# The last weight group, two stage borders and the order of weight splits in a float32 streaming block

## The chip, the cores and the metric

The kernel runs on one core of one Trainium2 chip. The metric is the device time of one execution in microseconds (us). The engines are TensorE (PE in the profile, with its weight load PEld), VectorE (DVE), ScalarE (ACT), GpSimd (POOL) and SyncE (SP); SP issues most DMAs, GpSimd those that add to their destination.

## The reference

One layer of a hybrid encoder block on x of 2048 rows and 1024 columns, in float32:

```python
h = rmsnorm(x, norm1_g)
u, p_rwkv, gate_a, gate_b = split(h @ W_in)            # gates through a sigmoid
o_a = s5_branch(u, ...);  o_b = rwkv7_branch(p_rwkv, ...)
merged = gate_a * (o_a @ Wb_a) + gate_b * (o_b @ Wb_b)
x = x + merged @ W_out                                 # phase C
h2 = rmsnorm(x, norm2_g)
x = x + square(relu(h2 @ W1)) @ W2                     # FF1 (W1: 1024x4096), FF2 (W2: 4096x1024)
out = rmsnorm(x, norm_f_g)
```

The change lies in the end of phase C, in FF1, FF2 and the final norm.

## The kernel before

**Split products.** TensorE multiplies in a format that keeps fewer bits than float32. Each operand is therefore split into a high part h (a cast on ScalarE) and the rest l (a subtraction on VectorE or GpSimd), and each product is three matmuls: l·h, h·l, h·h, lines L121, L122 and L123 of the helper `mm3`. Every 128x512 output block is collected in a PSUM bank.

**Phase C** runs over four windows of 512 rows. In a window the last part, n = 0 and 1, multiplies the merged branches by two halves of W_out, eight weight tiles each: loaded as `wor` (L1123), cast to `woh` (L1126), split to `wol` (L1127, GpSimd). During the last window's last part `following()` advances `FF1.ahead()` one step per weight tile: it loads FF1's first inputs, builds the combined activations (`early`, `build`, with casts `bh`) and splits the first weights.

**FF1** is a 2x2 scheme with seven products per block in place of eight (`ORD1` = 1, 5, 6, 2, 7, 3, 4). There are two halves of rows and 16 pairs of weight columns in each half, so pairs p = 0 to 31. A unit (p, i) is 12 matmuls into bank `f`. `weights()` walks the list `seq` of units three units ahead of TensorE: product i needs a sum or difference of the raw weight quarters `w1r` (L1339, VectorE, in place), then the cast `w1h` (L1342), then the split `w1l` (L1344; GpSimd for odd n and for the pairs at the halves' border, else VectorE). Pairs 0 and 1 alternate in `seq`; all others follow one after another. While p = 14 and 15 run, `build(1, …)` makes the activations of the second half, `bh` (ACT, L1314) and `bl` (DVE, L1315). Results are squared after a relu and written to the scratch `r_d`.

**FF2** (`phase_d2`) has eight groups g of W2 rows. Groups 0 to 6 use the same seven products (`ORD2` = 1, 5, 2, 6, 7, 3, 4), each with two halves s of rows: 98 units `s{g}_{i}` of 24 matmuls. `wsplit()` makes the weight of the next product one product ahead: a difference of raw quarters on VectorE, a cast `w2h` (L1508), a split `w2l` (L1509, VectorE). `asplit()` loads the activation pieces (`ra`, `ch`), casts them to `ah` (L1537, ACT) and splits them to `al` (L1538, GpSimd), three buffers deep. Some pieces are sums that accumulate DMAs from GpSimd make (L1481, L1486). `collect` adds a bank to one of the running sums s1, s5, s7, u, c11, c12, c21 (L1565, VectorE); for each row block j there is one tile of each, and c11 and c12 share the tile c0, c21 and s7 the tile c1. In group 0 some of them first add a part of x1, the phase-C result (L1561, L1562).

**Group 7** multiplies plainly, 4 quarters q of the output by 2 halves s, two weight pieces k each: banks `z`. `before(q, j)` adds the running sums together (helper `tt`, L1616) ahead of the takes (L1659), and then each row block is squared (`fj`, L1600), scaled (`rs`, L1605 to L1607 on GpSimd) and multiplied (`fin`, L1611, VectorE), and written out.

**Order.** A scheduler orders the recorded instructions of each engine; instructions passed to `keep_in_program_order` stay in the order of the code. SBUF is full, so raw tiles, splits and sums share numbered buffers (`tile4`).

Of the kernel before, what the change touches and what calls it, by code (L numbers as in the profile page):

```python
# [999 lines left out]
def phase_c(tc, nc, K, io, z_d, oa_d, ob_d, gt_d, x1_d, xt_d, following):  # L1000
    V, A, P, T = nc.vector, nc.scalar, nc.gpsimd, nc.tensor
    with ExitStack() as st:
# [141 lines left out]
        for w in range(NW):  # L1144
# [31 lines left out]
            for n in range(2):  # L1176
                po = [bank(f"o{w}_{n}_{i}", n) for i in range(4)]
                xs = []
                for k in range(8):
                    wh, wl = wq.pop(0)  # L1180
                    j = 8 * n + k + 2
                    if j < 16:
                        wq.append(loadw(j // 8, j % 8))
                    next(sp, None)
                    next(tn, None)
                    if k == 4:
                        late.flush()
                    if k >= 4:
                        i = k - 4
                        t0 = 512 * w + 128 * i  # L1190
                        xt = xp.tile([128, 512], F32, tag="xt", name=f"xt{w}_{n}_{i}", bufs=4)
                        nc.sync.dma_start(xt, io["x"][t0:t0 + 128, 512 * n:512 * n + 512])
                        xs.append(xt)
                    for i in range(4):
                        mm3(nc, po[i], mh[k][:, 128 * i:128 * i + 128], ml[k][:, 128 * i:128 * i + 128], wh, wl,
                            k == 0, k == 7)
                for i in range(4):
                    t0 = 512 * w + 128 * i
                    V.tensor_tensor(xs[i], xs[i], po[i], op=ALU.add)
                    jk = xp.tile([128, 512], F32, tag="jk", name=f"cj{w}_{n}_{i}", bufs=1)  # L1200
                    A.activation(jk, xs[i], ACTF.Square, accum_out=K.ss[:, n, 4 * w + i:4 * w + i + 1])
                    late.put(lambda t0=t0, n=n, xt=xs[i]: nc.sync.dma_start(
                        x1_d[t0:t0 + 128, 512 * n:512 * n + 512], xt))
# [4 lines left out]
        for _ in sp:  # L1208
            pass
        late.flush()  # L1210
# [30 lines left out]
class FF1:  # L1241
# [5 lines left out]
    def __init__(self, tc, nc, K, io, x1_d, xt_d, r_d, st, rp):  # L1247
# [5 lines left out]
        self.seq = [(p, i) for i in ORD1 for p in (0, 1)] + [(p, i) for p in range(2, 2 * NP1) for i in ORD1]  # L1253
# [4 lines left out]
    def tile4(self, i, n):  # L1258
        return self.rp.tile([128, 2, 512], F32, tag=f"r{i}", name=n)
# [39 lines left out]
    def build(self, half, s):  # L1299
# [3 lines left out]
        for i in ORD1:  # L1303
# [4 lines left out]
            for k in range(4):  # L1308
# [5 lines left out]
                A.copy(h[k], o)  # L1314
# [12 lines left out]
    def weights(self):  # L1327

        V, A, P = self.nc.vector, self.nc.scalar, self.nc.gpsimd
        for n, (p, i) in enumerate(self.seq):  # L1330
# [11 lines left out]
            A.copy(h, o)  # L1342
            edge = self.NP1 - 1 <= p <= self.NP1
            (P if n % 2 or edge else V).tensor_tensor(l, o, h, op=ALU.subtract)  # L1344
            if p < 2 and i == 4:
                self.wload(p + 2)
            elif p > 2 and i == 2:
                self.wload(p + 1)
            yield h, l

    def ahead(self):
# [13 lines left out]
        self.ring = []  # L1365
        for _ in range(self.AHEAD):
            self.ring.append(next(self.ws))
            yield

    def run(self, st, start):  # L1370
# [8 lines left out]
        def out(p, i, l, c):  # L1379

            pair, half, w = p % NP1, p // NP1, 2 * (p // NP1) + l
            E = V if NP1 - 1 <= p <= NP1 else P
# [71 lines left out]
def a_pieces(nc, io, r_d, tile4):  # L1454
# [4 lines left out]
    order += [(7, (q, k), s) for q in (0, 0, 1, 1) for s in range(2) for k in range(2)]  # L1459
# [6 lines left out]
    def load(n):  # L1466
# [7 lines left out]
        raw[n] = tile4(4 + turn[0] % 4, f"ra{n}")  # L1474
# [17 lines left out]
def phase_d2(tc, nc, K, io, x1_d, out, pieces, w2raw):  # L1492
# [5 lines left out]
    with ExitStack() as st:  # L1498
# [13 lines left out]
        def wsplit():  # L1512
            for g in range(7):
                r = w2raw(g)
                b11, b12, b21, b22 = r[0, 0], r[0, 1], r[1, 0], r[1, 1]
                for i in ORD2:
                    if i == 5:
                        V.tensor_tensor(b11, b12, b11, op=ALU.subtract)
                    elif i == 6:
                        V.tensor_tensor(b11, b22, b11, op=ALU.subtract)  # L1520
                    elif i == 7:
                        V.tensor_tensor(b12, b22, b12, op=ALU.subtract)
                    elif i == 4:
                        V.tensor_tensor(b21, b21, b11, op=ALU.subtract)
# [50 lines left out]
        for g in range(7):  # L1575
            for i in ORD2:
                wh, wl = wring.pop(0)
                wring.append(next(ws))
# [39 lines left out]
        def before(q, j):  # L1618
# [12 lines left out]
            if q == 2 and j < 6:  # L1631
                fin(0, j)
            if q == 3 and j in (0, 1):
                fin(0, 6 + j)
            if q == 3 and j >= 4:
                fin(1, j - 4)

        wk = wring + [next(ws)]
        for q in range(4):
            for s in range(2):  # L1640
                banks = [ps.tile([128, 512], F32, tag="s", name=f"z{q}_{s}{jj}") for jj in range(4)]
                for k in range(2):
                    if s == 1 and k == 1 and q < 3:
                        wk.append(next(ws))
                    if s == 0 and k == 0 and q > 0:
                        wk.append(next(ws))
                    wh, wl = wk[k]
                    ah, al = aring.pop(0)
                    for jj in range(4):
                        j = 4 * s + jj  # L1650
                        for b in range(2):
                            js = slice(128 * jj, 128 * jj + 128)
                            mm3(nc, banks[jj], ah[:, b, js], al[:, b, js], wh[:, b], wl[:, b],
                                k == 0 and b == 0, k == 1 and b == 1)
                        if k == 0:
                            before(q, j)
                            continue
                        d = quarters(j)[q]
                        V.tensor_tensor(d, d, banks[jj], op=ALU.add if q > 1 else ALU.subtract)  # L1659
                        if q == 0:  # L1660
                            square(0, j, 0)
                        elif q == 1:
                            square(0, j, 1)
                            if jj == 3:
                                scale(0, j - 3, 4)
                        elif q == 2:
                            square(1, j, 0)
                        else:
                            square(1, j, 1)
                            if s == 0 and jj == 3:  # L1670
                                scale(1, 0, 4)
                            elif s == 1:
                                scale(1, j, 1)
                                if jj:
                                    fin(1, j - 1)
                    anext()
            wk = wk[2:]
# [11 lines left out]
def phase_d(tc, nc, K, io, x1_d, r_d, out, s1, ff):  # L1689
# [21 lines left out]
    phase_d2(tc, nc, K, io, x1_d, out, pieces, w2raw)  # L1711
# [100 lines left out]
```

## Time and profile before

| | |
|---|---|
| median of 3 runs | 3162.46 us (3151.77 to 3171.28) |
| profiled execution | 3154.89 us, span 3153.1 us |
| mean granted TensorE clock | 0.966 |
| TensorE busy | 2928.6 us, 93% |
| VectorE busy | 1982.5 us, 63% |
| GpSimd busy | 1368.8 us, 43% |
| ScalarE busy | 1176.7 us, 37% |
| DMA traffic | 442.01 MB, mean 140 GB/s |

The span is the time between the first and the last recorded instruction; the profiled execution's own time is 1.8 us longer. Matmuls are shown pipelined, each with 0.39 us although one starts every 0.225 us at full clock, so a busy TensorE is read from the count of matmuls in a slice. A row of a group reads: line, engine, operation, output <- inputs, shape, count | busy us, mean ns of one | idle time of the engine just before them and what ended it.

### The profile page before, as it was taken

The numbers are of one execution on the slowest core, as the hardware profiler recorded it, in microseconds if no ns is written. First come the engines' busy times: TensorE is split into PE (matmuls) and PEld (weight loads), VectorE is DVE, ScalarE is ACT, GpSimd is POOL, SyncE is SP. The second block draws the span as 40 slices with busy tenths as digits, with TensorE's granted clock in tenths as the row PEclk, the third lists the DMA queues.
The fourth block names the chain that finished last, engine by engine and source line by source line (L and its number), as shares of the span: only waits on it lengthen the run. The fifth ranks groups of instructions, "written<-read, shape, count | busy, mean of one in ns | idle before, by whom it ended". The sixth has DMA issues, their size and how long they took to land.

```text
span 3153.1 us, 45632 instructions
## 1 busy us (share of the span) xinstructions
PE 2928.6 (93%) x17024; PEld 2336.5 (74%) x17024; DVE 1982.5 (63%) x3326; ACT 1176.7 (37%) x1855; POOL 1368.8 (43%) x1118
## 2 busy tenths in 40 slices
PE   7989999589899998999999899998999999999996
PEld 6757776467677776777877688886888778888874
DVE  6357884478777787535322556557566576666677
ACT  4442121233443433334444455545333432222232
POOL 3101101655564554323333355554544555555556
PEclk9999999789999998999999999998999999999998
DMA  4344444635344334257665643334333566666623
GB/s 146 96 138 135 136 139 138 190 96 153 94 116 153 95 96 128 78 135 232 192 214 168 213 151 120 112 113 154 124 110 108 186 175 153 154 154 150 150 88 127
DMA packets 319006, 442.01 MB, mean 140 GB/s; under 512 B 111936, under 2 KB 173504, under 8 KB 318784
## 3 DMA queue, kind: packets, MB, share of 16 engines
q1 hardware_dynamic: 294080, 405.54, 40.4%
q0 software_dynamic: 8064, 29.36, 5.4%
q10 hardware_dynamic: 16640, 4.20, 0.5%
q8 instruction: 134, 2.20, 0.3%
q14 instruction: 88, 0.72, 0.1%
HBM read 306.74 MB, written 131.07 MB: 139 GB/s over the span
## 4 chain that ended last, share of the span: by engine, by line
PE 45%; DMA 5%; DVE 4%; issue 2%; POOL 2%; ACT 2%; SPq 0%; POOLq 0%; ACTq 0%; DVEq 0%
PE f L123 6%; PE f L121 6%; PE f L122 6%; PE s L121 5%; PE s L122 5%; PE s L123 5%; DMA g<-gt_d 2%; PE o L121 1%; PE o L122 1%; PE o L123 1%; PE gp L121 1%; POOL w1l L1344 1%; PE gp L122 1%; PE gp L123 1%; DMA wor<-in_wout_dram 1%
## 5 line engine op out<-in xcount | busy, mean ns | idle before, releaser
L121 PE MATMUL f<-bl,w1h 128*128 128x512 f32 x896 | 354.0, 395 | 7.2 <-ACT w1h L1342 7.2
L122 PE MATMUL f<-bh,w1l 128*128 128x512 f32 x896 | 350.2, 391 | 8.0 <-POOL w1l L1344 7.9
L123 PE MATMUL f<-bh,w1h 128*128 128x512 f32 x896 | 351.9, 393 | 0.0
L121 PE MATMUL s<-w2l,ah 128*128 128x512 f32 x784 | 306.0, 390 | 8.4 <-DVE c L1408 4.9
L122 PE MATMUL s<-w2h,al 128*128 128x512 f32 x784 | 305.7, 390 | 0.0
L123 PE MATMUL s<-w2h,ah 128*128 128x512 f32 x784 | 305.6, 390 | 0.0
L1344 POOL TENSOR_TENSOR w1l<-w1r,w1h 128x512 fp32r<-128x512 f32 x119 | 177.5, 1493 | 193.6 <-ACT w1h L1342 187.5
L1538 POOL TENSOR_TENSOR al<-ra,ah 128x1024 fp32r<-128x1024 f32 x72 | 187.4, 2605 | 115.3 <-ACT ah L1537 111.0
L121 PE MATMUL gp<-gh,gwh 128*128 128x512 f32 x512 | 227.3, 444 | 10.8 <-DMA gh<-h_d 10.7
L1342 ACT CAST w1h<-w1r 128x512 fp32r<-128x512 f32 x224 | 138.4, 620 | 225.2 <-PE f L123 171.1
L122 PE MATMUL gp<-gh,gwl 128*128 128x512 f32 x512 | 213.4, 417 | 6.5 <-POOL gwl L959 6.5
L123 PE MATMUL gp<-gh,gwh 128*128 128x512 f32 x512 | 209.8, 410 | 0.0
L122 PEld LDWEIGHTS f<-bh,w1l 128*128 128x128 f32 x896 | 168.9, 189 | 46.6 <-POOL w1l L1344 9.7
L1565 DVE TENSOR_TENSOR c<-c,s 128x512 f32<-128x512 f32 x216 | 144.5, 684 | 91.1 <-PE s L123 91.1
L121 PEld LDWEIGHTS f<-bl,w1h 128*128 128x128 f32 x896 | 169.1, 189 | 42.8 <-ACT w1h L1342 8.3
L123 PEld LDWEIGHTS f<-bh,w1h 128*128 128x128 f32 x896 | 168.9, 188 | 38.4
L959 POOL TENSOR_TENSOR gwl<-gwr,gwh 128x1024 fp32r<-128x1024 f32 x64 | 153.5, 2398 | 97.7 <-ACT gwh L958 79.6
L121 PE MATMUL p<-hl,wh 128*128 128x512 f32 x448 | 182.6, 408 | 3.6 <-ACT lo L583 3.6
L123 PE MATMUL p<-hh,wh 128*128 128x512 f32 x448 | 178.3, 398 | 0.0
L122 PE MATMUL p<-hh,wl 128*128 128x512 f32 x448 | 177.9, 397 | 0.0
L121 PEld LDWEIGHTS s<-w2l,ah 128*128 128x128 f32 x784 | 147.6, 188 | 40.8 <-issue 6.6
L123 PEld LDWEIGHTS s<-w2h,ah 128*128 128x128 f32 x784 | 147.6, 188 | 30.7
(381 smaller groups left out, 7052.9 us busy)
## 6 DMA issues: line engine op xcount, KB each, us to landing
ra<-r_d SPq DMA_DIRECT2D x72, 512.0 KB, 3.4
gwr<-in_win_dram SPq DMA_DIRECT2D x64, 512.0 KB, 3.8
w1r<-in_w_dram SPq DMA_DIRECT2D x64, 512.0 KB, 3.4
r_d<-c SPq DMA_DIRECT2D x128, 256.0 KB, 2.0
ch<-r_d POOLq DMA_DIRECT2D x42, 512.0 KB, 5.5
gh<-h_d SPq DMA_DIRECT2D x64, 256.0 KB, 5.3
gt_d<-gs SPq DMA_DIRECT2D x64, 256.0 KB, 2.8
g<-gt_d SPq DMA_DIRECT2D x64, 256.0 KB, 3.4
```

The lines of the kernel that those rows point to most:

```text
L121: nc.tensor.matmul(ps, wh, xl, start=start, stop=False)
L122: nc.tensor.matmul(ps, wl, xh, start=False, stop=False)
L123: nc.tensor.matmul(ps, wh, xh, start=False, stop=stop)
L959: P.tensor_tensor(wl, wr, wh, op=ALU.subtract)
L1342: A.copy(h, o)
L1344: (P if n % 2 or edge else V).tensor_tensor(l, o, h, op=ALU.subtract)
L1538: P.tensor_tensor(l, raw[n], h, op=ALU.subtract)
L1565: V.tensor_tensor(d, d, bank, op=ALU.add if i in (4, 5, 6) else ALU.subtract)
```

## The change

It edits four places. The end of phase C: `ahead()` marks the place of the first weight splits with "weights"; phase C stops advancing there, and runs the rest after its own last work. The casts of `build` and the first weight casts keep program order. FF1's list: the first two pairs alternate in both halves, so 16 and 17 run together; the rule for the pairs at the border reaches one pair further. The weight differences of FF2's group 0 keep program order. Group 7: its four weight splits stay resident, so that each activation piece is split once for two quarters (8 splits in place of 16, and 8 loads fewer); the order is q, s, l; 24 adds become accumulate DMAs within SBUF, issued by GpSimd, and s7 += s5 moves from GpSimd to VectorE.

```diff
                     if j < 16:
                         wq.append(loadw(j // 8, j % 8))
-                    next(sp, None)
+                    if sp is not None and next(sp, "weights") == "weights":
+                        rest, sp = sp, None
...
-        for _ in sp:
+        late.flush()
+        for _ in rest:
             pass
-        late.flush()
...
-        self.seq = [(p, i) for i in ORD1 for p in (0, 1)] + [(p, i) for p in range(2, 2 * NP1) for i in ORD1]
+        self.seq = []
+        for h in range(2):
+            self.seq += [(NP1 * h + e, i) for i in ORD1 for e in range(2)]
+            self.seq += [(p, i) for p in range(NP1 * h + 2, NP1 * h + NP1) for i in ORD1]
...
-                A.copy(h[k], o)
+                self.tc.keep_in_program_order(A.copy(h[k], o))
...
-            A.copy(h, o)
-            edge = self.NP1 - 1 <= p <= self.NP1
+            cast = A.copy(h, o)
+            if n < self.AHEAD:
+                self.tc.keep_in_program_order(cast)
+            edge = self.NP1 - 1 <= p <= self.NP1 + 1
...
-        self.ring = []
-        for _ in range(self.AHEAD):
-            self.ring.append(next(self.ws))
-            yield
+        yield "weights"
+        self.ring = [next(self.ws) for _ in range(self.AHEAD)]
...
+                def first(ins):
+                    if g == 0:
+                        tc.keep_in_program_order(ins)
...
-                        V.tensor_tensor(b11, b12, b11, op=ALU.subtract)
+                        first(V.tensor_tensor(b11, b12, b11, op=ALU.subtract))
...
+        def wlast():
             r = w2raw(7)
-            for q in range(4):
-                for k in range(2):
-                    yield wpair(r[k, q % 2], f"7_{q}{k}")
+            for n, (k, l) in enumerate(((0, 0), (1, 0), (0, 1), (1, 1))):
+                h = wq.tile([128, 2, 512], F32R, tag="w2" + "hl"[n % 2], name=f"w27_{k}{l}")
+                A.copy(h, r[k, l])
+                lo = tile4((8, 9, 6, 7)[n], f"w27l_{k}{l}", F32R)
+                V.tensor_tensor(lo, r[k, l], h, op=ALU.subtract)
+                yield (k, l), (h, lo)
...
+        def dma_add(o, x):
+            nc.gpsimd.dma_start(o, x, accum_op=ALU.add)
...
-            if q == 0:
-                tt(V, u[j], u[j], s1[j])
-                tt(V, c11, c11, s1[j])
-            elif q == 1:
+            if (q, l) == (0, 0):
+                dma_add(u[j], s1[j])
+                dma_add(c11, s1[j])
+            elif (q, l) == (0, 1):
                 tt(V, s5[j], s5[j], u[j])
                 tt(V, c12, c12, s5[j])
-                tt(P, u[j], u[j], s7)
-            elif q == 2:
+                dma_add(u[j], s7)
+            elif l == 0:
                 tt(V, c21, c21, u[j])
-                tt(P, s7, s7, s5[j])
-            if q == 2 and j < 6:
+                tt(V, s7, s7, s5[j])
                 fin(0, j)
...
+                        take(q, l, j, banks[jj])
+                        if q and s:
+                            scale(1, j, 1)
+                            if jj:
+                                fin(1, j - 1)
+                        elif jj == 3:
+                            scale(q, j - 3, 4)
```

GpSimd's queue in phase C's last window, before. `wol0_5` is the split of the sixth weight tile of n = 0, `w1l1_1` FF1's weight split for pair 1, product 1:

```order
L1127 TENSOR_TENSOR wol0_4_16196<-wor0_4_16193,woh0_4_16195 128x512
L1344 TENSOR_TENSOR w1l1_1_16538<-w1r1_0_16143,w1h1_1_16537 128x512
L1344 TENSOR_TENSOR w1l1_5_16625<-w1r1_1_16145,w1h1_5_16624 128x512
L1127 TENSOR_TENSOR wol0_5_16222<-wor0_5_16219,woh0_5_16221 128x512
L1127 TENSOR_TENSOR wol0_6_16248<-wor0_6_16245,woh0_6_16247 128x512
L1127 TENSOR_TENSOR wol0_7_16272<-wor0_7_16269,woh0_7_16271 128x512
```

The same queue after the change, from the last weight tiles of phase C on:

```order
L1127 TENSOR_TENSOR wol1_7_16496<-wor1_7_16493,woh1_7_16495 128x512
L1206 TENSOR_TENSOR rq1_78<-ss1_77 128x4
L1207 TENSOR_SCALAR rq1_78<-rq1_78 128x4
L1208 TENSOR_TENSOR rq1_78<-rq1_78,mhalf_75 128x4
L1350 TENSOR_TENSOR w1l1_1_16571<-w1r1_0_16143,w1h1_1_16570 128x512
L1350 TENSOR_TENSOR w1l1_5_16625<-w1r1_1_16145,w1h1_5_16624 128x512
```

The two FF1 splits have moved from between `wol0_4` and `wol0_5` to behind the last `wol` and the three steps of the norm's scale.

VectorE's queue at the start of FF2, before: `w20_10` is a raw weight quarter, `w2l0_6` the weight split of product 6, `c02<-…,u2` an add of x1, `c00<-…,s0_2_0` the take of a bank of product 2:

```order
L1524 TENSOR_TENSOR w20_10_21672<-w20_10_21672,w20_00_21668 128x1024
L1561 TENSOR_TENSOR c02_22031<-c02_22031,u2_22030 128x512
L1562 TENSOR_TENSOR c12_22032<-c12_22032,u2_22030 128x512
L1561 TENSOR_TENSOR c03_22047<-c03_22047,u3_22046 128x512
L1562 TENSOR_TENSOR c13_22048<-c13_22048,u3_22046 128x512
L1561 TENSOR_TENSOR c04_22068<-c04_22068,u4_22067 128x512
L1562 TENSOR_TENSOR c14_22069<-c14_22069,u4_22067 128x512
L1565 TENSOR_TENSOR c00_21999<-c00_21999,s0_2_0_22235 128x512
L1509 TENSOR_TENSOR w2l0_6_22232<-w20_00_21668,w2h0_6_22231 128x1024
```

After the change, the rows around the same split:

```order
L1583 TENSOR_TENSOR c05_22084<-c05_22084,s0_2_5_22281 128x512
L1579 TENSOR_TENSOR c07_22116<-c07_22116,u7_22115 128x512
L1580 TENSOR_TENSOR c17_22117<-c17_22117,u7_22115 128x512
L1532 TENSOR_TENSOR w20_00_21668<-w20_11_21674,w20_00_21668 128x1024
L1583 TENSOR_TENSOR c06_22100<-c06_22100,s0_2_6_22289 128x512
L1583 TENSOR_TENSOR c07_22116<-c07_22116,s0_2_7_22297 128x512
L1534 TENSOR_TENSOR w20_01_21670<-w20_11_21674,w20_01_21670 128x1024
L1516 TENSOR_TENSOR w2l0_6_22232<-w20_00_21668,w2h0_6_22231 128x1024
L1516 TENSOR_TENSOR w2l0_7_22313<-w20_01_21670,w2h0_7_22312 128x1024
```

The split of product 6 stood behind the first take of product 2; it now stands behind the last, and behind the x1 adds of all eight row blocks.

GpSimd's queue in group 7, before, where `al100` and so on are activation splits:

```order
L1538 TENSOR_TENSOR al99_26070<-ra99_25898,ah99_26069 128x1024
L1538 TENSOR_TENSOR al100_26120<-ra100_25941,ah100_26119 128x1024
L1538 TENSOR_TENSOR al101_26162<-ra101_25979,ah101_26161 128x1024
L1538 TENSOR_TENSOR al102_26204<-ra102_26029,ah102_26203 128x1024
L1538 TENSOR_TENSOR al103_26250<-ra103_26067,ah103_26249 128x1024
```

After the change, `DMA u0<-c10` being the issue of an accumulate DMA that adds s7 (the second half of tile c1) to u:

```order
L1556 TENSOR_TENSOR al99_26058<-ra99_25898,ah99_26057 128x1024
L1556 TENSOR_TENSOR al100_26128<-ra100_25941,ah100_26127 128x1024
L1639 DMA u0_21998<-c10_22000 128x512
L1639 DMA u1_22014<-c11_22016 128x512
L1639 DMA u2_22030<-c12_22032 128x512
L1639 DMA u3_22046<-c13_22048 128x512
L1556 TENSOR_TENSOR al101_26249<-ra101_25979,ah101_26248 128x1024
L1556 TENSOR_TENSOR al102_26289<-ra102_26017,ah102_26288 128x1024
```

Four issues now stand ahead of al101, and four more (u4 to u7) ahead of al103. The sixteen issues for u += s1 and c11 += s1 stand among al90 to al94.

More of the change, by code (lines that the diff above doesn't have):

```diff
@@ L1458, in a_pieces @@
     order = [(g, i, s) for g in range(7) for i in ORD2 for s in range(2)]
-    order += [(7, (q, k), s) for q in (0, 0, 1, 1) for s in range(2) for k in range(2)]
+    order += [(7, (q, k), s) for q in range(2) for s in range(2) for k in range(2)]
     def blk(g, i, j, s):
@@ L1489, in a_pieces, with phase_d2 @@
     return raw, load, add, follow, len(order)
-def phase_d2(tc, nc, K, io, x1_d, out, pieces, w2raw):
+def phase_d2(tc, nc, K, io, x1_d, out, pieces, w2raw, tile4):
     V, A, P, T = nc.vector, nc.scalar, nc.gpsimd, nc.tensor
@@ L1638, in phase_d2 @@
-        wk = wring + [next(ws)]
-        for q in range(4):
-            for s in range(2):
[L1641 to L1648, printed above, removed]
+        w = {}
@@ new lines, in phase_d2, with wnext, product, take @@
+        wl_ = wlast()
+        def wnext():
+            n = next(wl_, None)
+            if n is not None:
+                w[n[0]] = n[1]
+        wnext()
+        wnext()
+        def product(q, l, s, jj, k, bank, a):
+            (ah, al), (wh, wl) = a, w[k, l]
+            for b in range(2):
+                js = slice(128 * jj, 128 * jj + 128)
+                mm3(nc, bank, ah[:, b, js], al[:, b, js], wh[:, b], wl[:, b], k == 0 and b == 0, k == 1 and b == 1)
+        def take(q, l, j, bank):
+            d = quarters(j)[2 * q + l]
+            V.tensor_tensor(d, d, bank, op=ALU.add if q else ALU.subtract)
+            square(q, j, l)
@@ new lines, in phase_d2 @@
+        for q in range(2):
+            for s in range(2):
+                pair = [aring.pop(0)]
+                for l in range(2):
+                    banks = [ps.tile([128, 512], F32, tag="s", name=f"z{q}{l}_{s}{jj}") for jj in range(4)]
+                    if l == 0:
+                        wnext()
+                        wnext()
+                        for jj in range(4):
+                            product(q, l, s, jj, 0, banks[jj], pair[0])
+                            before(q, l, 4 * s + jj)
+                        anext()
+                        pair.append(aring.pop(0))
+                        for jj in range(4):
+                            product(q, l, s, jj, 1, banks[jj], pair[1])
+                            take(q, l, 4 * s + jj, banks[jj])
+                        continue
@@ L1659, in phase_d2 @@
[L1659 to L1675, printed above, removed]
+                        for k in range(2):
+                            product(q, l, s, jj, k, banks[jj], pair[k])
+                            if k == 0:
+                                if q == 0:
+                                    before(q, l, j)
+                                elif s:
+                                    fin(1, jj)
@@ L1710, in phase_d @@
         ff.run(s1, start)
-    phase_d2(tc, nc, K, io, x1_d, out, pieces, w2raw)
+    phase_d2(tc, nc, K, io, x1_d, out, pieces, w2raw, ff.tile4)
 def setup(tc, nc, st, io):
```

40 lines of the change are left out of this document (16 added, 24 removed).

## The prediction

> **What bounds the kernel now.** First view: the page. TensorE is busy for 93% of the span and VectorE, second, for 63%.
>
> ```profile
> PE 2928.6 (93%) x17024; PEld 2336.5 (74%) x17024; DVE 1982.5 (63%) x3326; ACT 1176.7 (37%) x1855; POOL 1368.8 (43%) x1118
> ```
>
> So the change can win only where TensorE stands still. Second view: the table of 25-us slices (columns: length, busy time and instructions of PE, PEld, DVE, ACT, POOL, then granted clock, DMA share, GB/s). A full slice holds about 111 matmuls, one every 0.225 us.
>
> ```profile
> 1825.00:1850.00 25.00, 25.00 (x112) 20.70 (x111) 6.52 (x11) 9.83 (x21) 7.77 (x8) 1.00 0.48 156
> ...
> 1775.00:1800.00 25.00, 20.07 (x92) 16.13 (x90) 17.36 (x26) 12.00 (x21) 5.24 (x4) 1.00 0.84 309
> 1800.00:1825.00 25.00, 15.49 (x63) 12.50 (x64) 13.13 (x16) 11.40 (x23) 11.52 (x9) 0.73 0.43 144
> ...
> 2150.00:2175.00 25.00, 13.34 (x52) 9.29 (x50) 25.00 (x41) 17.17 (x32) 7.62 (x3) 0.81 0.48 155
> ...
> 3050.00:3075.00 25.00, 19.50 (x87) 15.80 (x85) 19.81 (x18) 7.46 (x13) 18.95 (x12) 0.97 0.26 88
> 3075.00:3100.00 25.00, 17.92 (x69) 14.08 (x70) 23.81 (x19) 5.73 (x11) 22.32 (x12) 0.83 0.29 107
> ```
>
> Three places fall short: phase C into FF1 (from 1775), the middle of FF1 (2150) and the last group (from 3050). The change touches each, and a fourth, the start of FF2 near 2510, which is nearly full. Third view, the waits in those four windows (total, times, longest):
>
> ```profile
> PE o L121 <- POOL wol L1127: 14.4, 1, 14.4
> ...
> PE f L121 <- ACT w1h L1342: 7.2, 2, 6.8
> PE f L122 <- POOL w1l L1344: 6.2, 2, 5.2
> ...
> PE s L121 <- DVE c L1565: 2.4, 2, 1.5
> ...
> PE s L121 <- DVE w2l L1509: 1.0, 1, 1.0
> ...
> PE z L121 <- DVE w2l L1509: 23.5, 3, 11.2
> ```
>
> They are ceilings: 14.4 us for the first place, 7.2 + 6.2 = 13.4 for the second, 23.5 for the last group. To each comes a short stretch after the stop in which matmuls run at half pace (clock 0.73 to 0.83 in those slices), and to the last what lies behind its last matmul. In FF2's start only 2.4 + 1.0 us can be won.
>
> **Last group: the large gain.** Its first matmul and its end:
>
> ```profile
> 3025.28 0.39 PE L121 MATMUL z<-w2l,ah 128*128 128x512 f32 x1
> ...
> 3142.37 0.68 DVE L1659 TENSOR_TENSOR c<-c,z 128x512 f32<-128x512 f32 x1
> ...
> 3145.44 1.28 DVE L1611 SCALAR_TENSOR_TENSOR c<-c,rs,nfg 128x1024 f32<-128x1024 f32 x1 [0.38 <-POOL rs L1607]
> ...
> 3147.71 1.28 DVE L1611 SCALAR_TENSOR_TENSOR c<-c,rs,nfg 128x1024 f32<-128x1024 f32 x1 [0.98 <-POOL rs L1607]
> ```
>
> 384 matmuls at 0.2268 us are 87.1 us: TensorE alone would end at 3112.4. VectorE ends at 3149.0, and 4.1 us of output transfer close the span. The group is held by VectorE and GpSimd, which slow each other; their groups in the window 3036 to 3153:
>
> ```profile
> L1538 POOL TENSOR_TENSOR al<-ra,ah 128x1024 fp32r<-128x1024 f32 x12 | 36.0, 3011 | 19.0 <-ACT ah L1537 19.0
> L1611 DVE SCALAR_TENSOR_TENSOR c<-c,rs,nfg 128x1024 f32<-128x1024 f32 x16 | 27.2, 1720 | 11.7 <-POOL rs L1607 11.6
> L1659 DVE TENSOR_TENSOR c<-c,z 128x512 f32<-128x512 f32 x32 | 20.6, 678 | 5.9 <-PE z L123 5.8
> L1616 POOL TENSOR_TENSOR c<-c,s 128x512 f32<-128x512 f32 x8 | 15.9, 2014 | 0.0
> L1616 POOL TENSOR_TENSOR u<-u,c 128x512 f32<-128x512 f32 x8 | 13.5, 1682 | 5.5 <-DVE s L1616 5.5
> L1616 DVE TENSOR_TENSOR c<-c,u 128x512 f32<-128x512 f32 x8 | 12.8, 1618 | 0.0
> L1509 DVE TENSOR_TENSOR w2l<-w,w2h 128x1024 fp32r<-128x1024 f32 x6 | 9.0, 1492 | 2.8 <-ACT w2h L1508 2.8
> ```
>
> Removed: 16 GpSimd adds (15.9 + 13.5 = 29.4 us), 8 of the 16 activation splits (24 us at 3.0), 4 of 8 weight splits (6 us at 1.49), and 16 VectorE adds of s1 (11 us at the take's 0.68, 26 at 1.62; most of them ran before the first take and held nobody). Added: 8 adds s7+=s5 on VectorE, and 24 accumulate issues on GpSimd.
>
> I let VectorE begin at 3036, 48 matmuls after 3025.28 (four takes may come some 4 us sooner). Its work from there is 16 final products (1.28), 32 takes and 32 adds (0.68), two splits (1.2): 66.5 us without collisions. The last four row blocks (7.8 of it) go one after another, because the new order puts each final product ahead of the next block's take: from a take's start to its final product's end is 3142.37 to 3146.7, 4.35 us each, 17.4 in all. The other 58.7 start at 3036. I add 6 us in which VectorE waits for the first scales, which now queue on GpSimd behind two splits, and 6 for collisions with the splits that remain (four at 1.7, which is what 2.95 us for a 1.2-us split below shows): 3036 + 58.7 + 12 = 3106.7, + 17.4 = 3124, + 4.1 = 3128. TensorE isn't the bound: its groups of 96 end at 3047, 3069, 3092 and 3114 with a stall of 1.5. Against 3153 that is **+25**; I take **+22.5**, since more could collide: 13 if half the 32 adds still take 1.5, 28 if almost none does.
>
> The 24 issues:
>
> ```profile
> L1486 POOL DMA_DIRECT2D ch<-r_d x28: 873/887/892, 2484.2 to 2980.4; - x28
> L1481 POOL DMA_DIRECT2D ch<-r_d x14: 863/882/1217, 2218.2 to 2930.4; - x14
> ...
> 3016.68 2.49 POOL L1538 TENSOR_TENSOR al<-ra,ah 128x1024 fp32r<-128x1024 f32 x1 [3.95 <-ACT ah L1537]
> ```
>
> I price one at 0.89 us, measured beside a working VectorE (bounds 0 and 1.22). These moved 512 KB from DRAM; the new ones move 256 KB inside SBUF, which no row shows. Four ahead of al101 and four ahead of al103 take 3.6 us each time; they and 3 us more fit before the split is needed. Sixteen among al90 to al94 take 14.2 us in the preceding group, where GpSimd idles about as long as it splits (the row above: 3.95 before 2.49) and al98 is done 6 us before its first use at 3025.28.
>
> The Trainium skill ("SBUF — State Buffer", "Who interferes with whom") says that a VectorE instruction with two SBUF inputs contends with GpSimd instructions that read SBUF, and infers that it leaves descriptor writing alone; the 0.89 us row agrees. The same page's "DVE blocks DMA" trap (620 ns alone, 3100 overlapped with a copy) would make each issue 3.1 us; that is the second rival's case, at 24 × 3.1 − 33 = 41 us lost.
>
> **Phase C into FF1.** w1l1_1 and w1l1_5 leave the queue ahead of wol0_5:
>
> ```profile
> 1806.35 1.13 ACT L1126 CAST woh<-wor 128x512 fp32r<-128x512 f32 x2
> ...
> 1806.52 1.72 POOL L1344 TENSOR_TENSOR w1l<-w1r,w1h 128x512 fp32r<-128x512 f32 x1 [1.88 <-ACT w1h L1342]
> 1808.20 2.94 POOL L1127 TENSOR_TENSOR wol<-wor,woh 128x512 fp32r<-128x512 f32 x2
> ...
> 1792.22 1.60 SPq L1123 DMA_DIRECT2D wor<-in_wout_dram  x2
> ...
> DMA to landing us min/median/max: 2.4/2.8/9.2
> ```
>
> TensorE waits until the first of these two splits ends, 1809.5. What is late next is the load: issued 1792.22, landing 9.2 later (the longest; the last line is the issue-to-landing time of the wor loads) = 1801.4; cast 0.6, split 1.5: 1803.5, **+6**. The pieces moved are paid at FF1's start, which today follows phase C without a gap. Then the first cast stands behind the last square and its split behind four adds on VectorE:
>
> ```profile
> 1843.82 0.64 ACT L1201 ACTIVATE cj<-xt 128x512 f32<-128x512 f32 x1
> ...
> 1851.90 6.37 POOL L1344 TENSOR_TENSOR w1l<-w1r,w1h 128x512 fp32r<-128x512 f32 x1 [5.69 <-ACT w1h L1342]
> ```
>
> Square to 1844.5, cast 0.6, split 0.7: 1845.8, some −2.8, and −1 for three GpSimd splits in a stretch where one took 6.37. Net **+2.5** (from −3, one such split in the way, to +7, the start hidden).
>
> **Middle of FF1.** Today TensorE runs out after 16_5 and waits for w1r16_6, which VectorE reaches at 2168.97, and whose split on GpSimd then collides:
>
> ```profile
> 2168.97 0.68 DVE L1339 TENSOR_TENSOR w1r<-w1r,w1r 128x512 f32<-128x512 f32 x1
> ...
> 2170.38 8.88 POOL L1344 TENSOR_TENSOR w1l<-w1r,w1h 128x512 fp32r<-128x512 f32 x3 [9.70 <-ACT w1h L1342]
> ...
> 2176.84 0.79 PE L122 MATMUL f<-bh,w1l 128*128 128x512 f32 x1 [5.17 <-POOL w1l L1344]
> ```
>
> With two pairs together TensorE has 16_1, 17_1 and 16_5, but 17_5 needs an add that now stands behind nearly the whole build of the second half on VectorE, which is busy 25.00 of 25 us here: about 2174, plus cast and split, restart near 2177 as today (2176.84). One unit more, 12 × 0.225 = 2.7 us, is done by then: **+2.5** (−3 with a lockout of the size seen, +6 if the splits are clean).
>
> **Start of FF2: a new wait.** Program order on VectorE for the weight differences puts w2l0_6 behind the adds that wait for x1 and behind the last takes of s0_2:
>
> ```profile
> 2510.66 1.23 DVE L1524 TENSOR_TENSOR w<-w,w 128x1024 f32<-128x1024 f32 x1
> ...
> 2518.22 2.95 DVE L1509 TENSOR_TENSOR w2l<-w,w2h 128x1024 fp32r<-128x1024 f32 x1
> ...
> 2532.09 1.27 DVE L1565 TENSOR_TENSOR c<-c,s 128x512 f32<-128x512 f32 x2
> ```
>
> Today it is ready at 2521.2, when s0_6 is due (near 2521.5: 48 matmuls of s0_2 from 2510.7). Afterwards VectorE runs the queue from 2510.66 to the takes' end at 2533.4 without the 1.2 of w20_10 and the 2.95, and with 1.2 for the difference of product 6: 2530.4; then the difference for product 7 and the split, 1.2 each: 2532.8. Nothing hides this: behind the split waits s0_6's first matmul, and behind that all of TensorE. It idles 11.3 us, wins back the 2.4 of bank waits (the takes are done by then), and loses some 1.5 at half pace: **−10** (−14 with one more collision and the slow stretch longer, −2 if x1 lands early enough for the adds to run ahead).
>
> **Sum.** 22.5 + 2.5 + 2.5 − 10 = 17.5: the profiled execution's 3154.9 (span 3153.1 and 1.8 around it) becomes 3137.4. It lies 0.24% under the median shown, 3162.5; on that scale 17.5 gives 3144.9; I say 3143, leaning a little to the walk's 25.
>
> **Rivals** (on the median's scale).
> 1. *The stops shrink and the FF2 queue costs little:* 28 + 6 + 5 − 2 = 37, 3125. For it: ceilings of 14.4 and 13.4; against it: the order of VectorE's queue.
> 2. *Issues locked out by VectorE, slower.* GpSimd's 24 accumulate issues each wait for VectorE. Sixteen ahead of al92 to al94 have some 20 us of room, eight ahead of al101 and al103 13 us (slack included); at x us each the loss is 24x − 33, which eats the 17.5 from x = 2.1. At 3 us, half the 6.37-us split above, it is 39: 3162.5 + 21 = 3184. Against it: 28 issues at 0.87 to 0.89.
> 3. *No net change:* the last group's end only passes from weights to VectorE (+13), FF2's wait at −12: with the other two at 0, 3161.
>
> **Chances.** Forecast 0.55 (its own range 3132 to 3155), rival 1 0.2, rival 3 0.19, rival 2 0.06. A measurement of this kernel can tell about 1%, 31.6 us, from no change: faster needs 3131 or less, which is rival 1 less a little; slower is most of rival 2. Faster 0.2, same 0.75, slower 0.05. The range reaches from beyond rival 1's centre to rival 3: 3118 to 3164.
>
> **What would show it.** The wait of z for w2l gone and the last matmul near 3114; the wait of o for wol cut from 14.4 to 8; a wait of f17_5 near 2165; a wait of s on w2l near 10 us instead of 1.0; accumulate issues near 0.9 us. Wrong if accumulate issues read 2 us or more, if s shows no such wait, or if FF1's start stalls beyond 6 us.

## The result and the profile after

| | before | changed |
|---|---|---|
| median | 3165.45 us (18 runs, 3151.77 to 3178.63) | 3146.71 us (18 runs, 3129.92 to 3156.49) |
| profiled execution | 3154.89 us, span 3153.1 | 3141.62 us, span 3139.8 |

The ratio is 0.9932, 95% interval 0.9915 to 0.9949: some 21 us faster. The whole interval lies below 1, so the gain is clear of the scatter of these 36 runs, though it is smaller than the 1% that the prediction called the limit of telling. Predicted were 3143 us and a gain of 17.5.

The page after, first line, and then the waits of TensorE in the four windows of the prediction (total, times, longest):

```profile
PE 2929.1 (93%) x17024; PEld 2337.3 (74%) x17024; DVE 1948.1 (62%) x3315; ACT 1165.1 (37%) x1843; POOL 1330.8 (42%) x1117
```

```profile
PE o L121 <- POOL wol L1127: 8.5, 1, 8.5
PE f L122 <- POOL w1l L1350: 3.3, 1, 3.3
PE f L121 <- ACT w1h L1346: 2.3, 1, 2.3
...
PE f L121 <- ACT w1h L1346: 11.4, 2, 11.0
PE f L122 <- POOL w1l L1350: 1.8, 2, 0.9
...
PE s L121 <- DVE w2l L1516: 15.7, 2, 8.5
PE s L121 <- DVE c L1415: 0.9, 1, 0.9
...
PE z L122 <- POOL al L1556: 0.2, 1, 0.2
```

Two waits of before that the prediction does not show, at FF1's start and at its end:

```profile
PE f L122 <- POOL w1l L1344: 1.7, 1, 1.7
...
PE s L121 <- DVE c L1408: 4.9, 1, 4.9
```

The 23.5 us of z on weights are gone, o waits 8.5 in place of 14.4, FF1's start waits 5.6 in place of 1.7, its middle 13.2 in place of 13.4. The first s waits 0.9 for FF1's last sums in place of 4.9, and s waits 15.7 on its weight splits in place of 1.0.

Waits leave out the half-paced matmuls behind them (0.79 us for the row behind the stop of 11.0 us, at 2181.26, in place of 0.39), so a second reading cuts the span at landmarks: first and last start of a group, from the view of one tile's instructions (minimum, median and maximum ns, then first and last start). Before, then changed:

```profile
L121 PE MATMUL o<-wol,mh x256: 387/389/794, 1491.5 to 1841.9; 128*128 128x512 f32 x128
L123 PE MATMUL o<-woh,mh x256: 387/389/628, 1492.0 to 1842.4; 128*128 128x512 f32 x128
L123 PE MATMUL f<-bh,w1h x896: 388/392/628, 1843.1 to 2480.8; 128*128 128x512 f32 x180
```

```profile
L121 PE MATMUL o<-wol,mh x256: 387/389/796, 1497.4 to 1841.8; 128*128 128x512 f32 x128
L123 PE MATMUL o<-woh,mh x256: 387/389/628, 1497.9 to 1842.3; 128*128 128x512 f32 x128
L123 PE MATMUL f<-bh,w1h x896: 388/392/628, 1846.0 to 2484.6; 128*128 128x512 f32 x180
L121 PE MATMUL z<-w27l,ah x128: 388/389/398, 3039.3 to 3126.4; 128*128 128x512 f32 x128
```

| stretch | before | changed | gain | predicted |
|---|---|---|---|---|
| start to first o (not touched) | 1491.5 | 1497.4 | −5.9 | 0 |
| first o to last o | 350.9 | 344.9 | +6.0 | +6 |
| last o to last f (FF1) | 638.4 | 642.3 | −3.9 | −3.5 at the start, +2.5 in the middle |
| last f to first z (groups 0 to 6) | 544.5 | 554.7 | −10.2 | −10 |
| first z to the end | 127.8 | 100.5 | +27.3 | +22.5 |
| sum | 3153.1 | 3139.8 | +13.3 | +17.5 |

The first row isn't the change: in the kernels below the first o starts between 1481.7 and 1505.9, with the same code ahead of it. These 24 us can account for most of the scatter of the times. So the four other rows are compared between single profiled executions; they add up to 19.2, near the ratio's 21.

**The last group after.** The groups from 3050 on:

```profile
L1631 DVE SCALAR_TENSOR_TENSOR c<-c,rs,nfg 128x1024 f32<-128x1024 f32 x16 | 20.2, 1280 | 20.0 <-POOL rs L1627 20.0
L1636 DVE TENSOR_TENSOR c<-c,s 128x512 f32<-128x512 f32 x16 | 13.2, 824 | 0.2
L1636 DVE TENSOR_TENSOR c<-c,u 128x512 f32<-128x512 f32 x8 | 7.5, 943 | 0.0
```

The final product takes 1.28 us in place of 1.72, the add of u 0.94 in place of 1.62: the collisions with GpSimd are mostly gone. VectorE, which I had bounding this group, idles 20 us for the scales. TensorE runs its 384 matmuls with one wait of 0.2 us, 3039.3 to 3126.9, and the rest is a tail of 12.9 us.

**The start of FF2.** VectorE's rows up to w2l0_2, the weight split of product 2, before:

```profile
2501.00 0.69 DVE L1561 TENSOR_TENSOR c<-c,u 128x512 f32<-128x512 f32 x1 [15.03 <-DMA u<-x_d]
2501.61 0.69 DVE L1562 TENSOR_TENSOR c<-c,u 128x512 f32<-128x512 f32 x1
2506.36 2.53 DVE L1561 TENSOR_TENSOR c<-c,u 128x512 f32<-128x512 f32 x1 [4.06 <-DMA u<-x_d]
2508.81 0.68 DVE L1562 TENSOR_TENSOR c<-c,u 128x512 f32<-128x512 f32 x1
2509.41 1.21 DVE L1509 TENSOR_TENSOR w2l<-w,w2h 128x1024 fp32r<-128x1024 f32 x1
```

VectorE's and TensorE's rows after:

```profile
2506.67 1.03 DVE L1579 TENSOR_TENSOR c<-c,u 128x512 f32<-128x512 f32 x1 [20.94 <-DMA u<-x_d]
2507.62 2.84 DVE L1580 TENSOR_TENSOR c<-c,u 128x512 f32<-128x512 f32 x1
2510.38 2.82 DVE L1579 TENSOR_TENSOR c<-c,u 128x512 f32<-128x512 f32 x1
2513.13 0.68 DVE L1580 TENSOR_TENSOR c<-c,u 128x512 f32<-128x512 f32 x1
2513.73 1.21 DVE L1516 TENSOR_TENSOR w2l<-w,w2h 128x1024 fp32r<-128x1024 f32 x1
...
2530.20 3.35 DVE L1532 TENSOR_TENSOR w<-w,w 128x1024 f32<-128x1024 f32 x1
...
2535.81 2.42 DVE L1516 TENSOR_TENSOR w2l<-w,w2h 128x1024 fp32r<-128x1024 f32 x2
...
2515.09 0.76 PE L121 MATMUL s<-w2l,ah 128*128 128x512 f32 x1 [7.17 <-DVE w2l L1516]
2537.08 0.80 PE L121 MATMUL s<-w2l,ah 128*128 128x512 f32 x1 [8.53 <-DVE w2l L1516]
```

There are two stops. The second, 8.5 us, is the one predicted: the difference for product 6 (L1532) stands behind the adds of x1, the split at 2535.81 behind the takes. The first, 7.2 us, I had not seen: w2l0_2 (2513.73) waits behind four adds of x1. The same four stood there before. What differs is the timing: counted from FF1's last matmul, TensorE is ready for w2l0_2 after 23.3 us (2515.09 − 7.17 − 2484.6) where it was 28.9 before (2510.77 − 1.04 − 2480.8), and x1 arrives after 22.1 us where it was 20.2.

### The profile page after: what moved, and what is told of

Read it like the earlier page. It is cut to its first block, busy times and chain, and to the rows that moved or that the text cites. A ratio compares the mean times of both kernels' runs of the same rounds, so it can differ in the third digit from the quotient of the medians.

```text
span 3139.8 us, 45586 instructions
## 1 busy us (share of the span) xinstructions
PE 2929.1 (93%) x17024; PEld 2337.3 (74%) x17024; DVE 1948.1 (62%) x3315; ACT 1165.1 (37%) x1843; POOL 1330.8 (42%) x1117
## 4 chain that ended last, share of the span: by engine, by line
PE 42%; DMA 6%; DVE 3%; issue 3%; POOL 3%; ACT 2%; SPq 0%; POOLq 0%; ACTq 0%; DVEq 0%
PE f L121 6%; PE f L123 6%; PE f L122 6%; PE s L121 5%; PE s L122 5%; PE s L123 5%; DMA g<-gt_d 2%; DMA wor<-in_wout_dram 2%; PE o L121 1%; PE o L122 1%; PE o L123 1%; PE gp L121 1%; POOL wol L1127 1%; PE gp L122 1%; PE gp L123 1%
## 5 line engine op out<-in xcount | busy, mean ns | idle before, releaser
L123 PE MATMUL f<-bh,w1h 128*128 128x512 f32 x896 | 351.9, 393 | 0.0
L121 PE MATMUL s<-w2l,ah 128*128 128x512 f32 x784 | 307.1, 392 | 16.6 <-DVE w2l L1516 15.7
L1556 POOL TENSOR_TENSOR al<-ra,ah 128x1024 fp32r<-128x1024 f32 x64 | 166.1, 2603 | 115.5 <-ACT ah L1555 115.2
```

The lines of the kernel that those rows point to most:

```text
L121: nc.tensor.matmul(ps, wh, xl, start=start, stop=False)
L123: nc.tensor.matmul(ps, wh, xh, start=False, stop=stop)
L1556: P.tensor_tensor(l, raw[n], h, op=ALU.subtract)
```

## The experiments

All stand beside runs of the kernel before; the ratio is to these, and "stretch" means a row of the table above.

**The pin of the weight differences.** The changed kernel, with group 0's differences free to be reordered:

```diff
                 def first(ins):
-                    if g == 0:
-                        tc.keep_in_program_order(ins)
+                    pass
```

> The changed kernel, with the weight differences of FF2's group 0 no longer held in program order. Theory (the pin costs about 10 us net): TensorE's waits of s for w2l, 15.7 us in the changed kernel, fall to 3 or less; the wait of the first s for FF1's last sums comes back from 0.9 to 4 to 5; from FF1's last matmul to the first z there are about 545 us in place of 555; the time is about 10 us below the changed kernel, 0.990 of before. Rival (the arrival of x1 sets these waits, the order does not): s still waits 10 us or more for w2l and the time stays.

Median 3133.31, ratio 0.9916 (0.9885 to 0.9947). Last f to first z: 543.8 us (3018.9 − 2475.1) against 554.7. The waits of s:

```profile
PE s L121 <- DVE c L1415: 4.9, 1, 4.9
PE s L121 <- DVE c L1582: 2.3, 2, 1.5
```

No wait for w2l is left, and the 4.9 us at FF1's end are back. The pin did win those 4 us, by letting FF1's last sums go ahead of two differences (VectorE's rows at 2476.76 and 2483.92 before), and lost them, with 11 more, behind it.

**The differences early, still pinned.** Those for products 6 and 7 are written behind the split of product 5:

```diff
+                    pair = wpair(...)
+                    if g == 0 and i == 5:
+                        first(V.tensor_tensor(b11, b22, b11, op=ALU.subtract))
+                        first(V.tensor_tensor(b12, b22, b12, op=ALU.subtract))
...
```

> The changed kernel, with the differences for products 6 and 7 of group 0 written right behind the split of product 5, still in program order. Theory: the second wait for w2l (8.5 us, w2l0_6) goes, since its difference no longer stands behind the eight adds of x1; the first (7.2 us, w2l0_2) stays, since that split still stands behind four adds of x1; some 2 of the 4 us won at FF1's end are given back, as these two differences stand ahead of FF1's last sums again: 5 to 7 us below the changed kernel. Rival (VectorE is simply too busy there): the wait of 8.5 moves to another split or to a bank and less than 3 us are won.

Median 3126.58, ratio 0.9908 (0.988 to 0.9936); the stretch is 543.9 (3017.0 − 2473.1). I expected the first wait to stay, and it went:

```profile
PE s L121 <- DVE c L1415: 4.9, 1, 4.9
PE s L121 <- DVE c L1587: 2.4, 2, 1.5
```

w2l0_2 stands behind the same four adds of x1 here. So the first wait is not made by the queue alone; it goes with how soon TensorE starts group 0. In the eight kernels of this document that start it 0.2 to 1.3 us after FF1's last matmul, x1 arrives 21.7 to 22.8 us after that matmul and TensorE stands 4.0 to 8.3 us at w2l0_2; in the six that start it after 5.3 to 5.4 us, x1 arrives after 19.1 to 20.2 and TensorE waits 1.0 or less. One of the eight, the interleaving alone (below), has no pin and waits 4.0. Why x1 arrives later in the eight was not tested.

The seven kernels with the change's pin, those further down included, have 554.7 to 555.9 us in this stretch, the seven others, this one among them, 543.5 to 544.5: the pin where the change puts it costs 11 us.

**The tail.**

```diff
-            V.scalar_tensor_tensor(a, a, rs[:, q, j:j + 1], nfg, op0=ALU.mult, op1=ALU.mult)
+            f = V.scalar_tensor_tensor(a, a, rs[:, q, j:j + 1], nfg, op0=ALU.mult, op1=ALU.mult)
+            if q and j >= 4:
+                tc.keep_in_program_order(f)
```

> The changed kernel, with the last four final products held in program order, so that the take of the next row block goes ahead of them. Theory (the serial chain take, square, scale, final product sets the tail, 3.9 us a block against TensorE's 2.7): the last VectorE instruction ends some 4.4 us after the last matmul in place of 9.0, and the span is 4 to 5 us shorter. Rival (ScalarE's and GpSimd's steps or the output's transfers set the tail): the distance stays near 9 us.

Median 3138.62, ratio 0.9933 (0.9908 to 0.9958); the time alone would not tell it from the changed kernel. The stretch does: 96.1 us (3136.8 − 3040.7) against 100.5. VectorE's last rows in the changed kernel, then here:

```profile
3126.84 1.28 DVE L1631 SCALAR_TENSOR_TENSOR c<-c,rs,nfg 128x1024 f32<-128x1024 f32 x1 [2.03 <-POOL rs L1627]
3128.04 0.68 DVE L1675 TENSOR_TENSOR c<-c,z 128x512 f32<-128x512 f32 x1
3130.74 1.28 DVE L1631 SCALAR_TENSOR_TENSOR c<-c,rs,nfg 128x1024 f32<-128x1024 f32 x1 [2.02 <-POOL rs L1627]
```

```profile
3126.67 1.28 DVE L1631 SCALAR_TENSOR_TENSOR c<-c,rs,nfg 128x1024 f32<-128x1024 f32 x1
3128.76 0.69 DVE L1677 TENSOR_TENSOR c<-c,z 128x512 f32<-128x512 f32 x1 [0.81 <-PE z L123]
3129.37 1.28 DVE L1631 SCALAR_TENSOR_TENSOR c<-c,rs,nfg 128x1024 f32<-128x1024 f32 x1
3131.64 1.28 DVE L1631 SCALAR_TENSOR_TENSOR c<-c,rs,nfg 128x1024 f32<-128x1024 f32 x1 [0.99 <-POOL rs L1627]
```

In the changed kernel each take waits for the final product ahead of it, a cycle of 3.9 us; here the last take waits for TensorE.

**Group 7 alone** on the kernel before: against the changed kernel the other three edits are taken back (a part of the diff is shown).

```diff
-                    if sp is not None and next(sp, "weights") == "weights":
-                        rest, sp = sp, None
+                    next(sp, None)
...
-        for h in range(2):
-            self.seq += [(NP1 * h + e, i) for i in ORD1 for e in range(2)]
...
-                    if g == 0:
-                        tc.keep_in_program_order(ins)
```

> The kernel before with only the change of group 7. Theory (the terms add): from the first z to the end of the span 100 to 101 us in place of 127.8, TensorE's wait of z for weights gone, everything ahead of it as before: 27 us below before, 0.9915, and 5 to 8 us below the changed kernel. Rival (the last group's gain hangs on the other edits, by the phase in which activation splits and VectorE meet): less than 20 us.

Median 3137.93, ratio 0.9923 (0.9896 to 0.995). First z to the end 100.6 us (3122.0 − 3021.4): the gain of group 7 stands by itself. By the time this one edit can't be told from all four together (0.9932). From the first o to the end it takes 1634.7 us (3122.0 − 1487.3) against the changed kernel's 1642.4 (3139.8 − 1497.4): in these two executions the other three edits together cost more than they won.

**Resident splits without the accumulate DMAs.** The 24 adds go back to VectorE and GpSimd:

```diff
-                dma_add(u[j], s1[j])
-                dma_add(c11, s1[j])
+                tt(V, u[j], u[j], s1[j])
+                tt(V, c11, c11, s1[j])
...
-                dma_add(u[j], s7)
+                tt(P, u[j], u[j], s7)
...
-                tt(V, s7, s7, s5[j])
+                tt(P, s7, s7, s5[j])
```

> The changed kernel with resident splits, but with the 24 accumulate DMAs made on VectorE (16 with s1) and GpSimd (8 with s7) again, and the 8 adds s7 += s5 on GpSimd, as before the change. Theory (both parts matter: fewer splits free GpSimd, and the adds on DMA free VectorE and its collisions): from first z to the end of the span 108 to 118 us, between 100.5 and 127.8. Rival 1 (resident splits are all of the gain): 103 or less. Rival 2 (the adds on DMA are all of it): 122 or more.

Median 3163.19, ratio 1.0 (0.9981 to 1.0019). First z to the end 112.4 us (3161.7 − 3049.3), TensorE waits 5.2 us for al, and GpSimd's adds are slow again:

```profile
L1636 POOL TENSOR_TENSOR u<-u,c 128x512 f32<-128x512 f32 x8 | 16.5, 2065 | 21.2 <-DVE s L1636 21.2
```

So 15 of the 27 us come with the resident splits and the new order of group 7, which this run can't part, and 12 with the adds on DMA. With the pin's 11 us against them, those 15 leave some 4 us, less than the interval of 6 us either way can show.

**The price of an accumulate issue.** Each accumulate DMA over 256 of 512 columns, so half of the addition is left out (one execution):

```diff
-            nc.gpsimd.dma_start(o, x, accum_op=ALU.add)
+            nc.gpsimd.dma_start(o[:, 0:256], x[:, 0:256], accum_op=ALU.add)
```

> The changed kernel, with each accumulate DMA of the last group over 256 of its 512 columns (half of the addition is left out). In the changed kernel the eight issues u += s1 took 3.0 us each on GpSimd, the eight u += s7 0.87. Theory (the issue waits for room in the queue, which drains by bytes): u += s1 falls to 1.5 us or less, and landing from 9.4 to 6 or less. Rival (VectorE locks GpSimd out, or the number of descriptors counts, which is the same): it stays at 2.5 to 3.5 us.

The GpSimd rows of the changed kernel, then of this one:

```profile
L1639 POOL DMA_DIRECT2D c<-s x8: 896/1780/2339, 2989.6 to 2998.7; - x8
L1639 POOL DMA_DIRECT2D u<-s x8: 915/3036/3425, 3001.6 to 3012.1; - x8
L1639 POOL DMA_DIRECT2D u<-c x8: 854/869/912, 3052.0 to 3085.4; - x8
```

```profile
L1639 POOL DMA_DIRECT2D u<-s x8: 2317/3506/4693, 2987.9 to 2994.2; - x8
L1639 POOL DMA_DIRECT2D u<-c x8: 854/869/912, 3037.8 to 3071.3; - x8
```

With half the bytes u += s1 lands sooner (a median of 7.4 us after the issue in place of 15.6; the 9.4 of the expectation is a median over other loads of u too), but its issue takes 3.5 us in place of 3.0: it isn't the queue's room. The rival's number came out, but not its cause. GpSimd's rows in time order in the changed kernel, and the sum of that stretch (columns as in the prediction's table; GpSimd is the fifth busy time):

```profile
2990.74 2.47 POOL L1639 DMA_DIRECT2D c<-s  x2
2991.86 3.79 POOL L1556 TENSOR_TENSOR al<-ch,ah 128x1024 fp32r<-128x1024 f32 x1
2994.21 2.28 POOL L1639 DMA_DIRECT2D c<-s  x1
...
2987.17:3017.76 30.59, 30.59 (x137) 25.33 (x135) 19.23 (x27) 7.20 (x8) 30.58 (x24) 1.00 0.99 211
```

The rows of issues and splits overlap: each is stretched while the other runs. In these 30.6 us GpSimd does 6 splits and 18 issues. At 2.45 us for a split and 0.885 for an issue, as such rows read where they stand apart, that is 14.7 + 15.9 = 30.6. With half the bytes the same 24 instructions take 30.7 us (2973.05 to 3003.71). So the issue's price is 0.89 us, as predicted; the 3.0 us are shared time. GpSimd was busy throughout, and TensorE (137 matmuls in 30.59 us) never waited.

**FF1's start.** The changed kernel, with the first two weight splits back in phase C's last two steps:

```diff
-        yield "weights"
-        self.ring = [next(self.ws) for _ in range(self.AHEAD)]
+        self.ring = [next(self.ws)]
+        yield
+        self.ring.append(next(self.ws))
+        yield "weights"
+        self.ring += [next(self.ws) for _ in range(2, self.AHEAD)]
```

> The changed kernel, with the first two of the three first FF1 weight splits (units 0_1 and 1_1) put back into the last two steps of phase C, behind the casts and splits of W_out's tiles. Theory (FF1's start waits because its first cast stands behind phase C's last square): the wait of f for w1h0_1, 2.3 us, goes, the half-paced matmuls behind it too, and the wait of o for wol stays near 7 to 8.5 us: 2 to 3 us less from the last o to FF1's third unit; the later wait of 3.3 us for a GpSimd split between VectorE's adds stays. Rival (the split of 1_1 on GpSimd is what is late): the wait only moves to the second unit and nothing is won.

Median 3146.33, ratio 0.9959 (0.9942 to 0.9976). The first wait goes, and the later one grows from 3.3 to 5.3; first o to last f is 686.0 us (2482.5 − 1496.5) against 687.2, while the other seven kernels with both FF1 edits lie between 686.5 and 691.2. So nothing is shown to be won, as the rival said, but not for its reason: the wait is not at the second unit, it is the later one behind a GpSimd split, at 1858.80 (1862.68 in the changed kernel).

```profile
PE f L122 <- POOL w1l L1350: 5.3, 1, 5.3
```

**The middle of FF1 and the transition apart.** Four kernels: the change without the interleaving; the kernel before with the interleaving alone; the kernel before with the transition alone; the change with the casts of `build` held in order in the first half only. The first, and the last:

```diff
-        for h in range(2):
-            self.seq += [(NP1 * h + e, i) for i in ORD1 for e in range(2)]
-            self.seq += [(p, i) for p in range(NP1 * h + 2, NP1 * h + NP1) for i in ORD1]
+        self.seq = [(p, i) for i in ORD1 for p in (0, 1)] + [(p, i) for p in range(2, 2 * NP1) for i in ORD1]
...
```

```diff
-                self.tc.keep_in_program_order(A.copy(h[k], o))
+                cast = A.copy(h[k], o)
+                if half == 0:
+                    self.tc.keep_in_program_order(cast)
```

> The changed kernel, with pairs 16 and 17 one after another again, and the border rules of before. Theory (one unit more is done by the same restart): TensorE's stop in the middle of FF1 goes back from one of 11.0 us to two of 6.8 and 5.2 us, and by 2250 us some 4 to 12 matmuls fewer are done, 1 to 2.7 us; the time stays within the noise of the changed kernel. Rival (the interleaving shortens the border by its own 13 us): 5 us or more are lost.

> The kernel before with only the edit of FF1's middle (pairs 16 and 17 together). From its last o to its last f the kernel before took 638.4 us, and the same stretch took 641 to 642 in six kernels with both FF1 edits, and 638.4 and 643.4 in two with the transition's edit alone. Theory A (the interleaving turns two stops into one of the same length and wins or loses nothing): 636 to 640 us, the time within 0.2% of before. Theory B (it costs, since both pairs now wait for the build): 641 or more. Theory C (it wins its unit, as predicted): 636 or less.

> The kernel before with only the edit of phase C's end. Theory (the wait for wol falls from 14.4 to 7 to 8.5 us, FF1's start pays 2.3 us and a collision): from first to last o 345 to 348 us in place of 351, from last o to last f 641 to 643 in place of 638.4 if the middle is not touched by the shift, 638 to 640 if the shift shortens the stop there: in all 2 to 6 us less than before, 0.998 to 0.999. Rival (the start pays back everything): no less than before.

> The changed kernel, with the build's casts kept in program order for the first half of FF1's activations alone. From last o to last f the transition's edit alone took 638.5 us, the middle's edit alone 637.0, both together 641 to 642. Theory (the two edits meet in the build of the second half, whose casts are held in order too, ahead of the cast for unit 17_5): the stop of 11.0 us falls to about 8 and the stretch to 637 to 639 us, 3 to 4 us below the changed kernel. Rival (it is the later start of FF1 that shifts the build against the units): the stop stays at 10.5 us or more and the stretch at 641 to 642.

| kernel | first to last o | last o to last f | longest stop in the middle | ratio |
|---|---|---|---|---|
| before | 350.9 | 638.4 | 6.8 | 1 |
| changed | 344.9 | 642.3 | 11.0 | 0.9932 |
| without interleaving | 348.0 | 638.4 | 6.1 | 0.995 (0.9926 to 0.9974) |
| interleaving alone | 351.4 | 637.0 | 8.0 | 0.9996 (0.9975 to 1.0016) |
| transition alone | 346.0 | 638.5 | 6.2 | 0.9983 (0.9958 to 1.0009) |
| casts in order in half 0 only | 348.3 | 642.9 | 8.0 | 0.9932 (0.9903 to 0.9961) |

The transition alone wins 5 us by its stretches, and FF1 takes no longer: its start waits 4.3 us in place of 1.7, its middle 9.4 in place of 13.4. Its time can't show it. Without the interleaving I expected the stops of 6.8 and 5.2 us back; the second came back with 1.1. The interleaving alone has a stretch 1.4 us shorter, which is too little to show: the kernel without the interleaving and the next section's kernel have the same FF1 code and take 638.4 and 643.4. With both edits FF1 takes 641 to 643 in all eight kernels here. The last kernel shows that the casts held in order lengthen the stop from 8 to 11 us, but its stretch is no shorter, where I had expected 3 to 4 us less: the waits of the middle still add up to 12.9 us against 13.2. A loss of some 3 us by the meeting of the two edits is likely, but with the 643.4 of a kernel without the interleaving it stays open.

**The terms together.** The change without its pin and without the interleaving, with the ordered tail (the three diffs above together):

> The changed kernel without the order of the weight differences, with pairs 16 and 17 one after another, and with the last four final products held in program order. Theory (the terms are independent and add): from last o to last f 638 to 639 us in place of 642, from there to the first z 544 in place of 555, from the first z to the end 96 in place of 100.5: 18 to 19 us below the changed kernel, near 3128 us, 0.988 of before or a little less. Rival (terms taken alone shift phases and eat each other): less than 12 us below the changed kernel.

Median 3125.99, ratio 0.988 (0.9855 to 0.9905). The interval lies below the changed kernel's (0.9915 to 0.9949), so it is faster than the kernel before and, by 0.5%, than the changed one; each of the two was timed beside its own runs of the kernel before. Last f to first z 544.0 (3027.8 − 2483.8), first z to the end 96.2 (3124.0 − 3027.8), as expected; FF1 took 643.4, not 638, so that term did not show.

## Why the prediction held, and where its steps did not

- **Sum.** 17.5 predicted, 19.2 measured between landmarks. That they agree is partly luck: the last group gave 4.8 us more than forecast, FF1 2.9 less, and the FF2 term came out at its size from other waits than the one forecast.
- **Last group, mis-sized: 22.5 against 27.3.** The step that failed is the allowance for collisions and the VectorE bound. The walk gave 25, and I took 2.5 off for further collisions (and the four that I counted at 1.7 us are 6.8, not 6). With no GpSimd adds left, only two of VectorE's adds collided (2.75 and 2.88 us in place of 0.68); the groups of adds and products ran at 0.7 to 0.9 and 1.28 us, VectorE kept up, and the bound passed to TensorE (87.6 us) and the serial tail. The tail's mechanism was right, its cycle 3.9 us in place of 4.35.
- **Accumulate issues.** I had written that 2 us or more for an issue would show the prediction wrong. Eight of the 24 rows do read 3.0 us in the median and eight more 1.8, but the sum shows that this sign was badly chosen: a row there holds time of a split too. The price of 0.89 us held, and rival 2 did not occur. u += s7 took 0.87 us beside VectorE's adds of two SBUF inputs (an issue from 3051.96 to 3052.84, an add from 3051.70 to 3052.39). The Trainium skill ("SBUF — State Buffer", "Who interferes with whom") infers that such adds leave descriptor writing alone; this trace agrees. The 3100 ns that the Trainium skill gives on the same page ("A bandwidth-pool intuition that's wrong (but worth ruling out)") are of a whole DMA beside a VectorE copy, a case that this stretch does not hold. The 3.0 us rows here are another thing, since they vanish in the sum.
- **Phase C, +6:** measured 6.0, and 4.9 with the edit alone. The ten kernels with this very edit have 344.6 to 348.3 us from first to last o, the three without it 350.9 to 351.9, so the gain is some 5 us and single executions give 3 to 7. FF1's start: the wait for the first cast was 2.3 where 2.8 was worked out; the GpSimd collision was 3.3 where 1 was (1.7 to 2.0 in seven other kernels with the edit, and 1.7 before).
- **Middle, +2.5:** 1.4 with the edit alone, within what the same code differs by, and nothing that can be shown in the whole change. From first o to last f, phase C and FF1 together, the changed kernel takes 687.2 us against 689.3, a gain of 2.1 that is not clear of those 686.5 to 691.2. The new stop at unit 17_5 is there, 11.0 us up to 2181.26; I had the restart at 2177.
- **FF2, −10:** measured −10.2, and 11 by the experiments, but not by the steps given. I forecast one stop of 11.3 us; there were two of 7.2 and 8.5, and 4 us won at FF1's end that no step of mine had. The step that failed is that I kept TensorE's and x1's times ahead of product 2 as they were: the four adds of x1 ahead of w2l0_2 were unchanged, but TensorE came to it 5.6 us sooner, and x1 1.9 us later, counted from FF1's end.

## What to carry to other kernels

An instruction held in program order is behind all that the program puts ahead of it, and here this included what waited for a transfer (the difference at 2530.20 behind the adds of x1): the pin that freed 4 us at one border brought waits of 15.7 at the next two stops. Price such an edit by its first wait that ends later, not by the one that goes. Where the time of a kernel scatters by more than an edit is worth, cut the span at landmarks on the bounding engine, and see from several executions how sharp each stretch is: groups 0 to 6 of FF2 agreed to 1 us over seven kernels, FF1 with the same code only to 5, and the medians of the kernel before, 3161.9 to 3167.1 us, differ by 5.

## What the runs showed of the hardware

- On GpSimd, the rows of DMA issues and of its own tensor instructions overlap and stretch each other (issue 0.90 to 3.4 us, split 2.5 to 4.9), while their sum stays: 6 × 2.45 + 18 × 0.885 = 30.6 us in 30.59.
- Half the bytes (128 KB for 256 KB) change neither an issue's price (0.87 us for u += s7 in both) nor that sum (30.7 us), only the landing (7.4 us in place of 15.6 for u += s1).
- In the changed kernel GpSimd issued 18 DMAs, at 0.885 us each, in a stretch in which VectorE was busy 19.23 of 30.59 us, and TensorE never waited.
